# A scatter of expert results in fp32r with a skipped second group, and four weight subtractions moved to VectorE

## The chip, the cores and the metric

The kernel runs on one core of a Trainium2 chip. The metric is the device time of one execution in microseconds (us); the time of a kernel is the median of several executions.

## The reference

A decoder trunk of two layers over one sequence of 256 tokens with 1024 channels, in fp32. Layer 0 is an input projection into q, k, v, a recurrent branch and its gate; differential attention with partial rotary embedding; a causal convolution with a gated linear recurrence; an output projection; and a dense SwiGLU of width 2816. Layer 1 is a pooling mixer and a mixture of eight SwiGLU experts of width 3584, of which each token uses two. The change concerns how the experts' results come back to their tokens:

```python
def moe_swiglu(h, router_w, wg, wu, wd):
    t = h.reshape(-1, dm)
    top_val, top_idx = lax.top_k((t @ router_w).astype(jnp.float32), TOP_K)
    gates = jax.nn.softmax(top_val, axis=-1)
    combine = jnp.sum(jax.nn.one_hot(top_idx, N_EXPERTS) * gates[..., None], axis=1)
    out = jnp.zeros_like(t)
    for e in range(N_EXPERTS):
        he = jax.nn.silu(t @ wg[e]) * (t @ wu[e])
        out = out + (combine[:, e:e + 1] * he) @ wd[e]
```

The result is the RMS norm of h plus this, times a gain.

## The kernel before

The weights are streamed in pieces of 128 partitions by 2048 columns (1 MB) by SyncE's DMA queue into a rotating set of buffers; `load_free` (L145) issues the next loads as soon as a buffer has been read for the last time.

**Layer 0, 0 to 330 us.** Matmuls of f32 weights run in three fp32r products: each half of a piece is split into hi (rounded to fp32r) and lo (the rest), `split_half` (L159): ScalarE makes hi (L167), and lo = raw - hi is a subtraction on VectorE or GpSimd (L168). `on_pool` (L155) chooses: the second halves (a = 1) of pieces 0 to 16 go to GpSimd where a caller doesn't name an engine, all others to VectorE. Pieces 0 to 9 are those of the input projection. Tile names in the order's rows carry a number: lo_197 is the second half of piece 1, lo_245 that of piece 2, lo_564 of piece 7, lo_629 of piece 8. The engines' instructions run in the order in which the program writes them (a schedule by hand), each engine its own queue, with semaphores between them.

Beside these products the first 107 us hold a chain of small steps. The row norms: squares on ScalarE, nine steps on 128x2 tiles on VectorE (`finish_rs`: L243, L223 to L230), `dg` (L283) for TensorE's `rsr` (L288), then `xb` (L402), the convolution (L409), the recurrence's gates (L419, L426), `lru_a` to `lru_d` (L436 to L450: GpSimd's product at L438, VectorE's at L442 and L446, scans at L450), the rotary products `rt` and `qk` (L464 to L468), transposes `qkT` (L477) and their copies to qT and kT (L480), then attention (scores from L494 on).

**Layer 1's experts, 330 to 1159 us.** Eight experts in seven pieces each, n = 7e + p. An expert's tokens lie in slots: a first group of 64 (`C0`), a second of 32 (`C1`); where an expert has more than 64 tokens, `big[e]` is set, read into a register of TensorE's queue. In piece n, TensorE runs the gate and up products of the first group (`mg`, L969, f32 tiles 128x64), under `tc.If(big[e])` those of the second group (`go`, L980, and `yo`, L1024, tiles of 128x32), else a matmul of one column (L991, bf16, so that the bank has a writer), then the down products of piece n - 1 (`y`, L1014) and transposes (`tp`, L1003). One piece reads six loads of 1 MB.

**The scatter.** After an expert's last piece `results(e)` (L1027) copies the sums of the second group (`yo`, VectorE) and the first (`y_`, ScalarE) to SBUF, into `ysb`. `gates(e)` (L938) builds for each token a row that holds its gate value at its slot (`selg`); `scatter_a` (L1031) transposes it (four 128x128) and copies it to `selT`. `scatter_b(t)` (L1042), for each half t of the tokens, multiplies the selection with the results, f32, 512 columns, in two row groups of 64 partitions (j = 0, 1, one for each half of the channels, each in its own bank), first the second group (m = 1), then the first (m = 0): four pairs. TensorE reads each f32 matmul as two instructions, so a call counts eight. `scatter_c` (L1049) adds the banks to the running output `ho` on VectorE. A table of jobs places these calls: gates and `scatter_a` in pieces 7e + 4 and 7e + 5, the two calls of expert e - 1's scatter in pieces 7e + 1 and 7e + 2 of the next expert, behind the first products of the piece (L1114 to L1119). There are 14 calls in the loop; the last expert's two stand behind the last down product (L1170), and behind them the final norm (`norm_out`, L1157): squares on ScalarE, nine small steps, four products on VectorE (L1167), four stores. `selg`, `selT` and `ysb` share one 1 MB buffer, `yt`.

Of the kernel before, what the change touches and what calls it, by code (L numbers as in the profile page):

```python
# [18 lines left out]
P = 128  # L19
# [8 lines left out]
E = 8  # L28
# [29 lines left out]
def hybrid_kernel(ctx, tc, x, cst, prm, row, gate, rtr, w_in, w_out, w_gu, w_dn, w_pool, m_gu, m_dn, out):  # L58
# [96 lines left out]
    def on_pool(i, a):  # L155

        return a and i < 17
# [757 lines left out]

    def more_room():


        yt = late.tile([P, W], F32, tag="band", name="yt")
        late_room.update(ysb=yt[:, 0:1024].rearrange("p (a c) -> p a c", a=2), selT=yt[:, 1024:1536].rearrange("p (a s) -> p a s", a=2),  # L920
                         selg=yt[:, 1536:2048].rearrange("p (t m s) -> p t m s", t=NT, m=2))
# [16 lines left out]
    def gates(e):  # L938
        for t in range(NT):
            for m, (a, c) in enumerate(((0, C0), (C0, C1))):  # L940
                dve.tensor_scalar(late_room["selg"][:, t, m].rearrange("p (o s) -> p o s", s=c),
                                  iota[:, a:a + c].rearrange("p (o s) -> p o s", o=1).to_broadcast([P, P // c, c]),
                                  pos[:, t, e:e + 1], cmb[:, t, e:e + 1], op0=OP.is_equal, op1=OP.mult)
# [38 lines left out]

    def more(parts):

        for e in sorted({n // EP for _, n in parts}):
            with tc.If(big[e] > 0, preferred_fallthrough_block=True) as c:
                for f, n in parts:
                    if n // EP == e:
                        f(n)
            with c.Else():  # L990
                pe.matmul(go[0:C1, 511:512], idb[:, 0:C1], idb[:, 0:1], start=True, stop=True)  # L991

    def hidden_a(n, b):
        sg = work.tile([P, 3, P], F32, name="sg", bufs=2)
        for v_, g_ in ((sg[:, 0:2], gates_of(b)), (sg[:, 2:3], gates_of(go[:, 0:2 * P]))):
            act.activation(v_, g_[:, :, 0, :], AF.Silu)  # L996
            dve.tensor_tensor(v_, v_, g_[:, :, 1, :], op=OP.mult)  # L997
        return sg

    def hidden_b(n, sg):  # L1000
        b = bank2("tp", "tp")
        for i in range(3):
            pe.transpose(b[:, i * P:(i + 1) * P], sg[:, i, :], ident)  # L1003
        het[n] = work.tile([P, 3, P], F32, name="het", bufs=2)
        act.copy(het[n].rearrange("p a c -> p (a c)"), b[:, 0:3 * P])  # L1005
# [21 lines left out]
    def results(e):  # L1027
        dve.tensor_copy(late_room["ysb"][:, 1], yo)
        act.copy(late_room["ysb"][:, 0], y_[e])

    def scatter_a():  # L1031

        b = misc("st")
        for t in range(NT):
            for m in range(2):
                pe.transpose(b[:, m * S + t * P:m * S + (t + 1) * P], late_room["selg"][:, t, m], ident)
        dve.tensor_copy(late_room["selT"].rearrange("p a s -> p (a s)"), b)
# [4 lines left out]
    def scatter_b(t, room=lambda name: misc(name)):  # L1042
        bs = [room(f"sc{t}{j}") for j in range(2)]
        for m in (1, 0):
            for j in range(2):
                pe.matmul(bs[j], late_room["selT"][j * C0:(j + 1) * C0, m, t * P:(t + 1) * P], late_room["ysb"][j * C0:(j + 1) * C0, m], start=m == 1, stop=m == 0)  # L1046
        return bs
# [41 lines left out]
    def scatter_next(t):  # L1089
        sc_[t] = scatter_b(t)  # L1090
# [14 lines left out]
    for e in range(E):  # L1105
        n = e * EP
        if e:
            do(n - 4, 2, gather_a, e)
            do(n - 3, 1, gather_next, e, 0)
            do(n - 3, 3, gathered, e, 0)  # L1110
            do(n - 2, 1, gather_next, e, 1)
            do(n - 2, 3, gathered, e, 1)
            do(n, 1, load_big, e)
            do(n + 1, 1, scatter_next, 0)  # L1114
            do(n + 1, 3, scattered, e - 1, 0)
            do(n + 2, 1, scatter_next, 1)
            do(n + 2, 3, scattered, e - 1, 1)
        do(n + 4, 0, gates, e)
        do(n + 5, 1, scatter_a)  # L1119
# [51 lines left out]
    bs = [scatter_b(0), scatter_b(1, lambda name: bank2("gu", name, 2))]  # L1171
# [10 lines left out]
    def rest_of(e, r):  # L1182
# [4 lines left out]
        for t in range(NT):  # L1187
            dve.tensor_scalar(s_[:, t, :], iota, pos[:, t, bass.ds(e, 1)], -float(CAP + r * P), op0=OP.subtract, op1=OP.is_equal)
            dve.tensor_scalar(late_room["selg"][:, t, 0], s_[:, t, :], cmb[:, t, bass.ds(e, 1)], None, op0=OP.mult)
# [4 lines left out]
        for t in range(NT):  # L1194
            pe.transpose(b[:, t * P:(t + 1) * P], late_room["selg"][:, t, 0], ident)
        dve.tensor_copy(late_room["selT"][:, 0], b[:, 0:S])
        with tc.For_i(0, EP, 1) as p:
# [7 lines left out]
            for c in range(2):  # L1205
                w = whole(m_dn[(e * EP + p) * 2 + c])
                sg = work.tile([P, 3, P], F32, tag="sg", name="sgo", bufs=2)[:, 0:2]
# [6 lines left out]
                ht = work.tile([P, 3, P], F32, tag="het", name="hto", bufs=2)[:, 0:2]  # L1214
                act.copy(ht, b[:, 0:2 * P].rearrange("p (a c) -> p a c", a=2))
                for j in range(2):
# [3 lines left out]
                    dve.tensor_add(y[:, j], y[:, j], b)  # L1220
        for t in range(NT):
            for j in range(2):
                b = misc(f"so{j}")
                pe.matmul(b, late_room["selT"][:, 0, t * P:(t + 1) * P], y[:, j], start=True, stop=True)
                hv = ho[0][:, t, j * 512:(j + 1) * 512]
                dve.tensor_add(hv, hv, b)
# [110 lines left out]
```

## Time and profile before

| | us |
|---|---|
| median of 3 runs (lowest, highest) | 1176.07 (1175.68, 1177.18) |
| profiled execution | 1175.88 |
| its span in the trace | 1173.9 |
| TensorE busy (share of the span) | 1133.8 (97%) |
| VectorE busy | 295.3 (25%) |
| ScalarE busy | 242.9 (21%) |
| GpSimd busy | 98.4 (8%) |
| chain of waits, by engine | TensorE 74%, DMA 18%, VectorE 4%, ScalarE 3% |

The profiled execution's time is 2.0 us longer than its span: what lies before the first and after the last instruction. Shares are averages over stages with different limits; the table by stages, the chain of waits and the timelines below separate them. In the rows, PE is TensorE, PEld its weight loads, DVE is VectorE, ACT ScalarE, POOL GpSimd; an arrow from a bracket names what ended the idle time before an instruction.

### The profile page before, as it was taken

The numbers are of one execution on the slowest core, as the hardware profiler recorded it, in microseconds if no ns is written. First come the engines' busy times: TensorE is split into PE (matmuls) and PEld (weight loads), VectorE is DVE, ScalarE is ACT, GpSimd is POOL, SyncE is SP. The second block draws the span as 40 slices with busy tenths as digits, with TensorE's granted clock in tenths as the row PEclk, the third lists the DMA queues.
The fourth block names the chain that finished last, engine by engine and source line by source line (L and its number), as shares of the span: only waits on it lengthen the run. The fifth ranks groups of instructions, "written<-read, shape, count | busy, mean of one in ns | idle before, by whom it ended". The sixth has DMA issues, their size and how long they took to land.

```text
span 1173.9 us, 16811 instructions
## 1 busy us (share of the span) xinstructions
PE 1133.8 (97%) x7071; PEld 582.5 (50%) x7071; DVE 295.3 (25%) x572; ACT 242.9 (21%) x491; POOL 98.4 (8%) x114
## 2 busy tenths in 40 slices
PE   7989999999999999998989999999999999999995
PEld 6867999999853333322323343333334433443331
DVE  6686664444731011111101100110010011001112
ACT  5756544444510010000000000000000000000011
POOL 2723151121200000000000000000000000000000
PEclk9999999999999999999999999999999999999998
DMA  9434956555899999999999999999999999999981
GB/s 353 149 124 141 391 182 213 173 187 180 306 372 415 419 415 419 416 416 419 415 421 415 418 415 415 419 402 420 416 418 407 415 421 415 419 363 417 418 350 38
DMA packets 69774, 408.67 MB, mean 348 GB/s; under 512 B 7844, under 2 KB 8104, under 8 KB 31400
## 3 DMA queue, kind: packets, MB, share of 16 engines
q1 hardware_dynamic: 69528, 407.08, 86.8%
q8 instruction: 80, 1.31, 0.5%
q10 hardware_dynamic: 144, 0.10, 0.1%
q14 instruction: 22, 0.18, 0.0%
HBM read 406.10 MB, written 1.05 MB: 347 GB/s over the span
## 4 chain that ended last, share of the span: by engine, by line
PE 74%; DMA 18%; DVE 4%; ACT 3%; issue 1%; DVEq 0%; ACTq 0%; SPq 0%
PE mg L969 26%; PE y L1014 12%; PE gu L185 11%; DMA raw<-in_m_gu 10%; PE go L980 6%; PE dn L185 5%; PE yo L1024 3%; DMA twohi<-in_m_gu 3%; DMA twolo<-in_m_gu 2%; PE sc L1046 2%; PE xe L951 2%; PE tp L1003 2%; DMA sparehl<-in_m_gu 1%; PE wo L185 1%; DMA spareh<-in_m_gu 1%; ACT hi L167 1%
## 5 line engine op out<-in xcount | busy, mean ns | idle before, releaser
L969 PE MATMUL mg<-raw,xe 128*64 128x512 f32 x928 | 219.0, 601 | 6.7 <-DMA raw<-in_m_gu 6.5
L997 DVE TENSOR_TENSOR sg<-sg,mg 128x256 f32<-128x256 f32 x56 | 23.6, 421 | 576.7 <-ACT sg L996 576.7
L996 ACT ACTIVATE sg<-mg 128x256 f32<-128x256 f32 x56 | 21.5, 383 | 564.7 <-PE mg L969 564.7
L168 DVE TENSOR_TENSOR lo<-raw,hi 128x1024 fp32r<-128x1024 f32 x80 | 99.9, 1269 | 95.6 <-ACT hi L167 95.4
L969 PEld LDWEIGHTS mg<-raw,xe 128*64 128x64 f32 x928 | 59.7, 136 | 123.1 <-issue 98.8
L167 ACT ACTIVATE hi<-raw 128x1024 fp32r<-128x1024 f32 x96 | 98.7, 1051 | 43.1 <-PE dn L185 28.5
L1014 PE MATMUL y<-raw,het 128*64 128x512 f32 x432 | 99.1, 593 | 1.1 <-DMA raw<-in_m_dn 1.1
L1014 PEld LDWEIGHTS y<-raw,het 128*64 128x64 f32 x432 | 30.7, 137 | 64.2 <-issue 57.0
L1005 ACT COPY het<-tp 128x384 f32<-128x384 f32 x56 | 26.8, 478 | 169.3 <-PE tp L1003 169.3
L969 PE MATMUL mg<-twohi,xe 128*64 128x512 f32 x212 | 55.2, 604 | 0.7 <-DMA twohi<-in_m_gu 0.7
L969 PE MATMUL mg<-twolo,xe 128*64 128x512 f32 x212 | 55.5, 602 | 0.4 <-DMA twolo<-in_m_gu 0.4
L1014 PE MATMUL y<-twohi,het 128*64 128x512 f32 x120 | 54.8, 593 | 0.5 <-ACT het L1005 0.5
L1014 PE MATMUL y<-twolo,het 128*64 128x512 f32 x120 | 54.7, 593 | 0.2 <-DMA twolo<-in_m_dn 0.2
L185 PE MATMUL gu<-xfl,hi 128*128 128x256 f32 x352 | 50.3, 283 | 0.0
L185 PE MATMUL gu<-xfh,hi 128*128 128x256 f32 x352 | 50.1, 283 | 0.0
L185 PE MATMUL gu<-xfh,lo 128*128 128x256 f32 x352 | 50.1, 283 | 0.0
L185 PEld LDWEIGHTS gu<-xfh,hi 128*128 128x128 f32 x352 | 46.2, 191 | 0.9
L185 PEld LDWEIGHTS gu<-xfl,hi 128*128 128x128 f32 x352 | 45.7, 192 | 0.2 <-DVE xfl L270 0.2
L185 PEld LDWEIGHTS gu<-xfh,lo 128*128 128x128 f32 x352 | 45.7, 192 | 0.0
L168 POOL TENSOR_TENSOR lo<-raw,hi 128x1024 fp32r<-128x1024 f32 x16 | 39.2, 2455 | 71.4 <-ACT hi L167 54.9
L969 PE MATMUL mg<-spare,xe 128*64 128x512 f32 x168 | 41.3, 602 | 2.7 <-DMA spare<-in_m_gu 2.7
L980 PE MATMUL go<-raw,xe 128*32 128x256 f32 x704 | 41.8, 380 | 0.0
(378 smaller groups left out, 1378.2 us busy)
## 6 DMA issues: line engine op xcount, KB each, us to landing
raw<-in_m_gu SPq DMA_DIRECT2D x116, 1024.0 KB, 17.8
raw<-in_m_dn SPq DMA_DIRECT2D x54, 1024.0 KB, 18.7
twohi<-in_m_gu SPq DMA_DIRECT2D x53, 512.0 KB, 13.8
twolo<-in_m_gu SPq DMA_DIRECT2D x53, 512.0 KB, 12.6
raw<-in_w_gu SPq DMA_DIRECT2D x22, 1024.0 KB, 4.8
spare<-in_m_gu SPq DMA_DIRECT2D x21, 1024.0 KB, 15.7
twohi<-in_m_dn SPq DMA_DIRECT2D x30, 512.0 KB, 13.8
twolo<-in_m_dn SPq DMA_DIRECT2D x30, 512.0 KB, 12.3
```

Of the source, the lines that this page charges most:

```text
L167: act.activation(hi, r, AF.Copy)
L168: eng.tensor_tensor(lo, r, hi.bitcast(F32), op=OP.subtract)
L185: pe.matmul(dst, l, r, start=start, stop=stop)
L951: pe.matmul(v_[:, k], h[:, t, (4 * k4 + k) * P:(4 * k4 + k + 1) * P], s_[:, t, :], start=t == 0, stop=t == NT - 1)
L969: pe.matmul(b[c * C0:(c + 1) * C0], x_[:, k, 0:C0], block(MOE[n] + k // 2, (k % 2 * 2 + c) * 512), start=k == 0, stop=k == 1)
L980: pe.matmul(go[q:q + C1, 0:2 * P], x_[:, k, C0:CAP], block(MOE[n] + k // 2, (k % 2 * 2 + c) * 512 + r * 2 * P, 2 * P), start=k == 0, stop= ...
L997: dve.tensor_tensor(v_, v_, g_[:, :, 1, :], op=OP.mult)
L1003: pe.transpose(b[:, i * P:(i + 1) * P], sg[:, i, :], ident)
L1005: act.copy(het[n].rearrange("p a c -> p (a c)"), b[:, 0:3 * P])
L1014: pe.matmul(y_[e][j * C0:(j + 1) * C0], het[n][:, r, c * C0:(c + 1) * C0], block(DOWN[n] + c, (2 * j + r) * 512), start=p == c == r == 0, ...
L1024: pe.matmul(yo[q:q + C1], het[n][:, 2, (2 * c + r) * C1:(2 * c + r + 1) * C1], block(DOWN[n] + c, (2 * j + r) * 512), start=p == r == 0, s ...
L1046: pe.matmul(bs[j], late_room["selT"][j * C0:(j + 1) * C0, m, t * P:(t + 1) * P], late_room["ysb"][j * C0:(j + 1) * C0, m], start=m == 1, s ...
```

## The change

Two independent edits.

1. `on_pool` no longer takes pieces 1, 2, 7 and 8: four subtractions go from GpSimd's queue to VectorE's, in the place where `split_half` is called.
2. The scatter. The selection `selT` becomes an exact 0 or 1 in fp32r (`is_gt` of the transposed gate rows); each slot's gate value is a sum over its row (`gsl`). `results` multiplies y by it and makes an fp32r hi half (ScalarE) and lo half (VectorE, `halve` at L209). `scatter_b` multiplies in fp32r, one instruction for a matmul: first group hi, then, under an If on `big[e]`, second group hi and lo, else the matmul of one column, then first group lo. `selg` and `selT` move to a pool of their own, `ysb` takes all of `yt`, and `sg` and `het` go from two buffers to one. The path for experts of more than 96 tokens changes in the same way (left out below).

```diff
     def on_pool(i, a):
 
-        return a and i < 17
+        return a and i < 17 and i not in (1, 2, 7, 8)
...
+    selg = work.tile([P, NT, 2, P], F32, name="selg", bufs=1)
+    selT = work.tile([P, 2, S], F32R, name="selT", bufs=1)
+
     def more_room():
 
-
-        yt = late.tile([P, W], F32, tag="band", name="yt")
-        late_room.update(ysb=yt[:, 0:1024].rearrange("p (a c) -> p a c", a=2), selT=yt[:, 1024:1536].rearrange("p (a s) -> p a s", a=2),
-                         selg=yt[:, 1536:2048].rearrange("p (t m s) -> p t m s", t=NT, m=2))
+        late_room.update(ysb=late.tile([P, W], F32R, tag="band", name="yt").rearrange("p (u a c) -> p u a c", u=2, a=2))
...
+    def where_big(e, f):
+        with tc.If(big[e] > 0, preferred_fallthrough_block=True) as c:
+            f()
+        with c.Else():
+            pe.matmul(go[0:C1, 511:512], idb[:, 0:C1], idb[:, 0:1], start=True, stop=True)
+
...
     def hidden_a(n, b):
-        sg = work.tile([P, 3, P], F32, name="sg", bufs=2)
+        sg = work.tile([P, 3, P], F32, name="sg", bufs=1)
...
-        het[n] = work.tile([P, 3, P], F32, name="het", bufs=2)
+        het[n] = work.tile([P, 3, P], F32, name="het", bufs=1)
...
     def results(e):
-        dve.tensor_copy(late_room["ysb"][:, 1], yo)
-        act.copy(late_room["ysb"][:, 0], y_[e])
-
-    def scatter_a():
+        for m, b in ((1, yo), (0, y_[e])):
+            hi, lo = (late_room["ysb"][:, u, m] for u in range(2))
+            halve(hi, lo, b, gsl[e][:, m:m + 1])
+
+    gsl = {}
+
+    def scatter_a(e):
 
         b = misc("st")
         for t in range(NT):
             for m in range(2):
-                pe.transpose(b[:, m * S + t * P:m * S + (t + 1) * P], late_room["selg"][:, t, m], ident)
-        dve.tensor_copy(late_room["selT"].rearrange("p a s -> p (a s)"), b)
+                pe.transpose(b[:, m * S + t * P:m * S + (t + 1) * P], selg[:, t, m], ident)
+        gsl[e] = work.tile([P, 2], F32, name="gsl", bufs=2)
+        dve.tensor_reduce(gsl[e], b.rearrange("p (a s) -> p a s", a=2), axis=AX.X, op=OP.add)
+        dve.tensor_scalar(selT.rearrange("p a s -> p (a s)"), b, 0.0, None, op0=OP.is_gt)
...
-    def scatter_b(t, room=lambda name: misc(name)):
+    def scatter_b(e, t, room=lambda name: misc(name)):
         bs = [room(f"sc{t}{j}") for j in range(2)]
-        for m in (1, 0):
+
+        def part(m, u, start=False, stop=False):
             for j in range(2):
-                pe.matmul(bs[j], late_room["selT"][j * C0:(j + 1) * C0, m, t * P:(t + 1) * P], late_room["ysb"][j * C0:(j + 1) * C0, m], start=m == 1, stop=m == 0)
+                rows_ = slice(j * C0, (j + 1) * C0)
+                pe.matmul(bs[j], selT[rows_, m, t * P:(t + 1) * P], late_room["ysb"][rows_, u, m], start=start, stop=stop)
+
+        part(0, 0, start=True)
+        where_big(e, lambda: [part(1, u) for u in range(2)])
+        part(0, 1, stop=True)
         return bs
```

The first two of the four subtractions on VectorE, the difference between the orders (- before, + after), near the start:

```order
 L270 SCALAR_TENSOR_TENSOR xml<-xt_171,pr,xmh 128x256 x2
 L168 TENSOR_TENSOR lo_189<-raw_97,hi_188 128x1024
+L168 TENSOR_TENSOR lo_197<-raw_97,hi_196 128x1024
 L243 SCALAR_TENSOR_TENSOR nwt<-ssq 128x2
 L223 TENSOR_SCALAR rs<-nwt 128x2
...
 L283 TENSOR_SCALAR dg<-pr,rs 128x128 x2
 L168 TENSOR_TENSOR lo_229<-raw_103,hi_228 128x1024
+L168 TENSOR_TENSOR lo_245<-raw_103,hi_244 128x1024
 L402 TENSOR_TENSOR xb<-x_155,rsr 128x256
 L402 TENSOR_TENSOR xb<-x_156,rsr 128x256
```

lo_197 now stands ahead of the nine small steps of the row norm (left out between them), lo_245 ahead of the first channels of the recurrent branch; in both places GpSimd's queue loses the same row. The other two, around the copies of q and k (`th`, `cv`: the recurrence; `rt`: the rotary products):

```order
 L480 COPY qT<-qkT_546 128x512
+L168 TENSOR_TENSOR lo_564<-raw_264,hi_563 128x1024
 L442 SCALAR_TENSOR_TENSOR th<-ri,th 128x1024
 L464 TENSOR_TENSOR rt<-qk,cs 128x128
...
 L446 TENSOR_TENSOR cv<-cv,th 128x1024
+L168 TENSOR_TENSOR lo_629<-raw_343,hi_628 128x1024
 L450 SCALAR_TENSOR_TENSOR th<-la,cv 128x256 x4
```

lo_564 stands ahead of both rotary products of k, lo_629 between them and the scans. TensorE's queue at the first scatter call of the loop, in the kernel after (before, the four L1046 matmuls of sc stand between the same mg rows, with no branch):

```order
L970 MATMUL mg_4189<-raw_3880,xe_3407 64x512 x2
L1055 MATMUL sc_4192<-yt,selT 128x512
L1055 MATMUL sc_4193<-yt,selT 128x512
L985 COMPARE_AND_BRANCH
L1055 MATMUL sc_4192<-yt,selT 128x512
L1055 MATMUL sc_4193<-yt,selT 128x512
L1055 MATMUL sc_4192<-yt,selT 128x512
L1055 MATMUL sc_4193<-yt,selT 128x512
L985 UNCONDITIONAL_BRANCH
L988 LDWEIGHTS idb
L988 MATMUL go<-idb 32x1
L985 UNCONDITIONAL_BRANCH
```

Either the four matmuls behind the compare run or the one of L988; the last pair (the lo half of the first group) and the next mg products follow behind the last row.

## Rows read from the trace of the kernel before

**Rows 1.** Table by stages: stretch, length, busy us by engine, clock, DMA share, GB/s.

```profile
0.00:107.00 107.00, 94.99 (x519) 79.21 (x520) 77.08 (x132) 69.33 (x141) 46.54 (x56) 0.97 0.55 197
107.00:330.00 223.00, 222.79 (x1554) 206.71 (x1552) 126.01 (x193) 106.48 (x162) 51.85 (x59) 0.99 0.65 234
...
739.00:826.00 87.00, 85.59 (x407) 29.85 (x406) 10.82 (x28) 7.73 (x22) 0.00 (x0) 1.00 1.01 414
826.00:1020.00 194.00, 193.59 (x1512) 74.40 (x1514) 18.53 (x48) 12.35 (x35) 0.00 (x0) 1.00 1.01 416
```

**Rows 2.** Chain of waits, pieces in order of time: start us, us, what.

```profile
145.04 5.62 PE dn L185 x24
...
826.41 1.94 PE mg L969 x8
...
837.87 1.92 PE sc L1046 x8
...
856.33 1.92 PE sc L1046 x8
```

**Rows 3.** Waits of TensorE, 0 to 107 us: total us, times, longest.

```profile
PE rsr L288 <- DVE dg L283: 2.9, 1, 2.9
PE qkT L477 <- DVE qk L468: 2.7, 1, 2.7
```

**Rows 4.** VectorE, timeline 16.9 to 25.2 us: start us, us, instruction, [idle before].

```profile
18.09 0.16 DVE L227 SCALAR_TENSOR_TENSOR nwt<-rs 128x2 f32<-128x2 f32 x1
18.29 2.26 DVE L228 TENSOR_TENSOR nwt<-nwt 128x2 f32<-128x2 f32 x1
...
23.08 0.48 DVE L283 TENSOR_SCALAR dg<-pr,rs 128x128 f32<-128x128 f32 x2
23.48 1.22 DVE L168 TENSOR_TENSOR lo<-raw,hi 128x1024 fp32r<-128x1024 f32 x1
25.06 0.43 DVE L402 TENSOR_TENSOR xb<-x,rsr 128x256 f32<-128x256 f32 x1 [0.37 <-ACT rsr L289]
```

**Rows 5.** Timeline of GpSimd (POOL), 16.9 to 64.9 us.

```profile
18.10 4.73 POOL L168 TENSOR_TENSOR lo<-raw,hi 128x1024 fp32r<-128x1024 f32 x2 [17.27 <-ACT hi L167]
...
53.48 3.40 POOL L438 TENSOR_TENSOR cv<-cv,ri 128x1024 f32<-128x1024 f32 x1
...
61.02 2.34 POOL L168 TENSOR_TENSOR lo<-raw,hi 128x1024 fp32r<-128x1024 f32 x1 [0.82 <-ACT hi L167]
```

**Rows 6.** Timeline of VectorE, 53 to 72 us.

```profile
57.89 2.46 DVE L464 TENSOR_TENSOR rt<-qk,cs 128x128 f32<-128x128 f32 x1
...
60.86 0.28 DVE L464 TENSOR_TENSOR rt<-qk,cs 128x128 f32<-128x128 f32 x1
61.06 2.52 DVE L467 TENSOR_TENSOR rt<-qk,cs 128x64 f32<-128x64 f32 x2
```

**Rows 7.** Timeline of ScalarE, 10 to 26 us.

```profile
16.98 2.93 ACT L167 ACTIVATE hi<-raw 128x1024 fp32r<-128x1024 f32 x3
```

**Rows 8.** Timeline of TensorE's weight loads (PEld), 1094.4 to 1096.6 us.

```profile
1094.50 0.30 PEld L1046 LDWEIGHTS sc<-yt 64*128 64x128 f32 x4 [0.81 <-issue]
...
1096.41 0.20 PEld L969 LDWEIGHTS mg<-raw,xe 128*64 128x64 f32 x4 [0.76 <-issue]
```

**Rows 9.** The same view, 1099.4 to 1103 us.

```profile
1100.76 0.14 PEld L969 LDWEIGHTS mg<-raw,xe 128*64 128x64 f32 x2 [0.28 <-issue]
1101.71 0.09 PEld L991 LDWEIGHTS <-idb 128*32 128x32 bf16 x1 [0.81 <-issue]
1101.82 0.20 PEld L969 LDWEIGHTS mg<-raw,xe 128*64 128x64 f32 x4
```

**Rows 10.** Timeline of ScalarE from 1158 us on.

```profile
1158.69 0.58 ACT L1029 COPY yt<-y 128x512 f32<-128x512 f32 x1 [3.75 <-PE y L1014]
```

**Rows 11.** Timeline of VectorE from 1158 us on.

```profile
1160.59 1.28 DVE L1054 TENSOR_TENSOR ho<-ho,sc 128x512 f32<-128x512 f32 x2 [5.39 <-PE sc L1046]
1162.31 1.28 DVE L1054 TENSOR_TENSOR ho<-ho,sc 128x512 f32<-128x512 f32 x2 [0.43 <-PE sc L1046]
```

More of the change, by code (lines that the diff above doesn't have):

```diff
@@ L940, in gates @@
             for m, (a, c) in enumerate(((0, C0), (C0, C1))):
-                dve.tensor_scalar(late_room["selg"][:, t, m].rearrange("p (o s) -> p o s", s=c),
+                dve.tensor_scalar(selg[:, t, m].rearrange("p (o s) -> p o s", s=c),
                                   iota[:, a:a + c].rearrange("p (o s) -> p o s", o=1).to_broadcast([P, P // c, c]),
@@ L981, in gate_up_more @@
                               start=k == 0, stop=k == KD - 1)
+    def where_big(e, f):
[3 more added lines that the diff above has]
+            pe.matmul(go[0:C1, 511:512], idb[:, 0:C1], idb[:, 0:1], start=True, stop=True)
     def more(parts):
         for e in sorted({n // EP for _, n in parts}):
[L986 to L991, printed above, removed]
+            where_big(e, lambda: [f(n) for f, n in parts if n // EP == e])
     def hidden_a(n, b):
-        sg = work.tile([P, 3, P], F32, name="sg", bufs=2)
+        sg = work.tile([P, 3, P], F32, name="sg", bufs=1)
         for v_, g_ in ((sg[:, 0:2], gates_of(b)), (sg[:, 2:3], gates_of(go[:, 0:2 * P]))):
@@ L1087, in gathered, with scatter_next @@
         gather_c(xe[e % 2], k4, gb_[k4])
-    def scatter_next(t):
-        sc_[t] = scatter_b(t)
+    def scatter_next(e, t):
+        sc_[t] = scatter_b(e, t)
     def scattered(e, t):
@@ L1113, in hybrid_kernel @@
             do(n, 1, load_big, e)
-            do(n + 1, 1, scatter_next, 0)
+            do(n + 1, 1, scatter_next, e - 1, 0)
             do(n + 1, 3, scattered, e - 1, 0)
-            do(n + 2, 1, scatter_next, 1)
+            do(n + 2, 1, scatter_next, e - 1, 1)
             do(n + 2, 3, scattered, e - 1, 1)
         do(n + 4, 0, gates, e)
-        do(n + 5, 1, scatter_a)
+        do(n + 5, 1, scatter_a, e)
     do(N - 1, 1, late_gains)
@@ L1170, in hybrid_kernel @@
     results(E - 1)
-    bs = [scatter_b(0), scatter_b(1, lambda name: bank2("gu", name, 2))]
+    bs = [scatter_b(E - 1, 0), scatter_b(E - 1, 1, lambda name: bank2("gu", name, 2))]
     for t in range(NT):
@@ L1188, in rest_of @@
             dve.tensor_scalar(s_[:, t, :], iota, pos[:, t, bass.ds(e, 1)], -float(CAP + r * P), op0=OP.subtract, op1=OP.is_equal)
-            dve.tensor_scalar(late_room["selg"][:, t, 0], s_[:, t, :], cmb[:, t, bass.ds(e, 1)], None, op0=OP.mult)
+            dve.tensor_scalar(selg[:, t, 0], s_[:, t, :], cmb[:, t, bass.ds(e, 1)], None, op0=OP.mult)
             dve.tensor_scalar(s_[:, t, :], s_[:, t, :], rs1[:, t:t + 1], None, op0=OP.mult)
@@ L1194, in rest_of @@
         for t in range(NT):
-            pe.transpose(b[:, t * P:(t + 1) * P], late_room["selg"][:, t, 0], ident)
-        dve.tensor_copy(late_room["selT"][:, 0], b[:, 0:S])
+            pe.transpose(b[:, t * P:(t + 1) * P], selg[:, t, 0], ident)
+        gs = work.tile([P, 2], F32, tag="gsl", name="gso", bufs=2)
+        dve.tensor_reduce(gs[:, 0:1], b[:, 0:S], axis=AX.X, op=OP.add)
+        dve.tensor_scalar(selT[:, 0], b[:, 0:S], 0.0, None, op0=OP.is_gt)
         with tc.For_i(0, EP, 1) as p:
@@ L1206, in rest_of @@
                 w = whole(m_dn[(e * EP + p) * 2 + c])
-                sg = work.tile([P, 3, P], F32, tag="sg", name="sgo", bufs=2)[:, 0:2]
+                sg = work.tile([P, 3, P], F32, tag="sg", name="sgo", bufs=1)[:, 0:2]
                 g_ = gates_of(bs[c])
@@ L1213, in rest_of @@
                     pe.transpose(b[:, i * P:(i + 1) * P], sg[:, i, :], ident)
-                ht = work.tile([P, 3, P], F32, tag="het", name="hto", bufs=2)[:, 0:2]
+                ht = work.tile([P, 3, P], F32, tag="het", name="hto", bufs=1)[:, 0:2]
                 act.copy(ht, b[:, 0:2 * P].rearrange("p (a c) -> p a c", a=2))
@@ L1220, in rest_of @@
                     dve.tensor_add(y[:, j], y[:, j], b)
+        halve(late_room["ysb"][:, 0], late_room["ysb"][:, 1], y, gs[:, 0:1])
         for t in range(NT):
@@ L1223, in rest_of @@
                 b = misc(f"so{j}")
-                pe.matmul(b, late_room["selT"][:, 0, t * P:(t + 1) * P], y[:, j], start=True, stop=True)
+                for u in range(2):
+                    pe.matmul(b, selT[:, 0, t * P:(t + 1) * P], late_room["ysb"][:, u, j], start=u == 0, stop=u == 1)
                 hv = ho[0][:, t, j * 512:(j + 1) * 512]
```

## The prediction, before the changed kernel ran

> **What bounds the kernel now.** The page says that TensorE has work for nearly the whole span, so the first question is where that work is the limit and where it merely fits beside something else. The table by stages answers it [rows 1]: from 107 to 330 us TensorE has work in 222.79 of 223.00 us at 0.65 of the DMA engines, so that a microsecond saved in the stage before arrives at 330 unchanged. From 739 to 826 us and on to 1020 the DMA share is above 1.00, at 414 to 416 GB/s: there the weights come as fast as they can. The chain of waits then says where the one limit takes over from the other [rows 2]: its last DMA piece ends at 826.41, and from there to the end it is TensorE with a short tail on ScalarE and VectorE. What TensorE saves ahead of 826 it spends waiting for the same bytes; what it saves behind 826 counts in full. The same view prices the two kinds of matmul: the f32 scatter call of eight takes 1.92 us, and 24 fp32r matmuls of 512 columns in L185 take 5.62 us, which is 0.234 each. Last, the waits of TensorE in the first 107 us name only two long ones on VectorE, 2.9 us at rsr (L288) and 2.7 us at qkT (L477) [rows 3]; the timelines of VectorE and GpSimd show why.
>
> **Part one: four subtractions from GpSimd to VectorE.** At 18.09 us a 128x2 step of the rms chain takes 0.16 us; the next, at 18.29, takes 2.26, and the one behind it as much, so that dg (L283), for which TensorE waits, starts at 23.08 [rows 4]. GpSimd runs two L168 subtractions from 18.10 for 4.73 us [rows 5]; by the order these are lo_197 and lo_245. The pattern comes back at 57.89 us, where one 128x128 product takes 2.46, and at 61.06, where two of 128x64 take 2.52, while the 128x128 product at 60.86 takes 0.28 [rows 6]; the next two subtractions of GpSimd, lo_564 and lo_629, lie over them, the second from 61.02 [rows 5]. So four blocks of 2.1 to 2.2 us leave VectorE's line, and four subtractions of 1.22 us (unblocked, as at 23.48 [rows 4]) enter it.
>
> Step by step: (a) lo_197 now stands ahead of nwt (L243) and adds a wait on ScalarE: its hi half is the first of three that start at 16.98 and take 2.93 [rows 7], done near 18.0. Queued behind the waiting instruction are the rms steps, dg, and with it TensorE. It runs from 18.1 to 19.3, nine small steps at 0.2 follow, and dg starts at 21.1 instead of 23.08: 2.0 earlier. (b) lo_245 stands ahead of xb (L402): 21.1 + 0.4 (dg) + 1.22 (lo_229) + 1.22 = 24.0 against 25.06: xb is 1.1 earlier. TensorE's wait at rsr shrinks by 2.0; the convolution behind xb, which feeds the gates and the long row of activations on ScalarE ahead of qT, gains only 1.1. (c) lo_564 stands behind GpSimd's own L438 (53.48, 3.40 us [rows 5]), which will block it as it now blocks L442; it costs 1.22, and two blocks of 2.2 go: qk (L468), for which qkT waits, comes 1.1 + 4.4 - 1.2 = 4.3 earlier at the most. (d) lo_629 takes 1.22 again, ahead of the scans and of the copy of kT: from there the lead is 3.1. What is late next is the attention behind kT, which waits for VectorE and ScalarE; GpSimd's later subtractions stay as they are. I take **3.0 us** for this part. The upper end is both waits of rows 3 less what (a) leaves, 2.0 + 2.7 = 4.7; the lower end is the lead of xb alone, 1.1, should something else hold kT back. The lead goes through 107 to 330 unchanged; behind that each load is issued when a buffer comes free, so that the stretch bound by DMA moves as a whole.
>
> **Part two: the scatter.** A call spans 1.92 us from its first weight load (1094.50) to the next one of mg (1096.41) [rows 8]: 0.10 until the first matmuls, four pairs (two row groups side by side) at 0.43, and 0.10 before tiles of another shape may load. The new call has fp32r pairs. Taking 0.234 for a pair, as for one matmul of L185, a call of an expert with a second group is 0.10 + 4 x 0.234 + 0.10 = 1.14, which is 0.78 less. Without one it is the pair for hi, the tiny matmul of the Else, and the pair for lo. The same filler in L991 costs 0.10 for the change of shape and 0.11 until the next load (1100.76 to 1101.71 is two pairs plus 0.10, then 1101.82 [rows 9]), so the call is 0.43 + 0.11 + 0.43 = 0.97, which is 0.95 less. Behind 826 lie six calls in the loop: two of an expert without the second group (837.87 and 856.33 [rows 2]) and four of experts with one, the last at 1094.50 [rows 8]; the rows of go (L980) say which experts those are. 2 x 0.95 + 4 x 0.78 = **5.0 us**. Does the first of them run into a late load? Two pieces with a call are 856.33 - 837.87 = 18.5 us apart, while six loads of 1 MB (6.29 million bytes) at 416 GB/s take 15.1. The lead over the loads, nothing at 826.41, is thus some 3 us when the first call ends, and 0.95 is taken from it. The eight calls ahead of 826 gain nothing: the loads of the stretches at a full DMA share cover them, and without that cover they would give up to 0.95 each.
>
> No row shows fp32r in tiles of 64 rows. If its two row groups ran one behind the other, a call would be 0.97 + 0.47 = 1.44 or 1.14 + 0.94 = 2.08: 2 x 0.48 - 4 x 0.16 = 0.3 us. I take side by side, since the nearest row, the f32 pair in the same tiles, runs so; 0.3 stays as the lower end.
>
> Each call now crosses an If. The filler's rows hold the crossing of the If in each piece as well, and beyond the change of shape they show nothing for it: at 1101.71 the compare has been worked off ahead of the matmuls. [...]
>
> **Part three: the tail.** The last call waits for ScalarE's copy of y, from 1158.69 for 0.58 [rows 10], and the first addition starts at 1160.59 [rows 11]. Now hi takes that copy's place; lo follows on VectorE for some 0.65 (as one addition of rows 11), to about 1160.0, beside the hi pair and the filler; the lo pair ends near 1160.45, and the second tile's by 1161.1 instead of 1162.31. The four additions then run without the pause of 0.43, but the squares on ScalarE behind them take up part of it: **0.3 us**, with 0.5 and -0.7 (hi, lo and filler all in series) as ends.
>
> The added halves in the loop (two activations for one, two subtractions for one copy, per expert) sit on engines that have work for a tenth of that time [rows 1], and TensorE asks for them a piece later. The single buffers of sg and het cost nothing: the transposes and products that read the old content stand earlier on TensorE. Without that cover each would be a wait of some 0.5 us per piece.
>
> **Sum:** 3.0 + 5.0 + 0.3 = 8.3 us. The profiled execution took 1175.88, 0.2 below the median of 1176.07; on the median that is 1167.8 us.
>
> **Rivals.** (1) The row groups of fp32r don't overlap: 3.0 + 0.3 + 0.3 = 3.6, so 1172.5. For it: fp32r occurs nowhere in such tiles. Against: f32 pairs overlap fully [rows 8]. (2) VectorE becomes the bound of the first stage: what the blocks give back goes to the subtractions and to ScalarE's row, and part one is worth 0 to 0.5: 1170.6. For it: VectorE has work in 77 of the first 107 us [rows 1]. Against: 8.7 us of blocks go and 4.9 of work come. [...] (3) The loads bind behind 826 as well, and part two is worth nothing: 1172.8. Against: the lead of 3 us. (4) **Slower:** the If in the middle of a call has one pair ahead of it where the If of a piece has a dozen, and TensorE's queue runs dry there. From (8.3 + 2.4) / 8 = 1.3 us for a crossing on, the eight crossings (six, and two at the end) make the kernel slower; at 2 us it is 16 - 8.3, so 1183.8. For it: no row shows an If under so little work. Against: the crossings that are shown cost nothing [rows 9].
>
> **Chances.** Forecast 0.60, (1) 0.13, (2) 0.13, (3) 0.07, (4) 0.07, of which half is slower by over 0.2% (2.4 us, what a measurement of this kernel can tell from no change). The low end takes the upper ends, 4.7 + 5.0 + 0.5 = 10.2, so 1165.9, and 0.4 for the spread of the runs: 1165.5. The high end takes in (1) to (3): 1173.0. Faster 0.88: the forecast, (2), and most of (1) and (3), which lie 0.9 to 1.2 inside the bound of 1173.7. Same 0.08, slower 0.04.
>
> **What would show it.** Right: no 128x2 step over 0.2 us between 18 and 21 us; dg at about 21.1; the wait at qkT under 0.5; the same TensorE work 3 us earlier at 330; scatter calls of about 1.0 and 1.15 us; no DMA in the chain behind about 823. Wrong: a call of 1.4 us or more (1), dg or kT as late as now (2), waits on DMA behind 826 (3), a gap at the If (4).

## The result and the profile after

| | before | after |
|---|---|---|
| median, us (runs; lowest, highest) | 1176.14 (4; 1175.68, 1177.18) | 1168.46 (4; 1165.94, 1168.91) |
| profiled execution, its span | 1175.88, 1173.9 | 1168.91, 1166.8 |

The ratio of after to before is 0.9925, with a 95% interval of 0.9912 to 0.9938: faster, by 7.7 us between the medians (8.8 by the ratio), where 8.3 were forecast. The time lies in the range, 0.7 us over the forecast. How it comes about is less tidy than the sum: one term came out larger, one as worked out, and two stretches at a granted clock of 0.50 took part of it back in the execution that was profiled. One execution of the kernel before, beside the last experiments, took 1636.21 us at a granted clock of 0.65 and is in no comparison.

The table by stages of the changed kernel, cut where the work is the same as in [rows 1] (columns as there):

```profile
0.00:102.00 102.00, 91.63 (x520) 75.16 (x521) 73.32 (x136) 69.43 (x141) 35.31 (x52) 0.98 0.56 207
102.00:325.00 223.00, 222.10 (x1554) 206.29 (x1551) 126.04 (x193) 106.41 (x162) 51.81 (x59) 1.00 0.65 235
...
823.00:1020.00 197.00, 197.00 (x1592) 76.80 (x1590) 20.92 (x51) 13.64 (x37) 0.00 (x0) 1.00 1.02 417
```

The first stage is 5 us shorter for the same work (0.9 of it the start of this execution, see below). GpSimd is busy 11.2 us less in it and VectorE 3.8 less, although it took over four subtractions: what it no longer spends blocked is more than it got. The waits of TensorE in the first 107 us, answering to [rows 3]:

```profile
PE qkT L477 <- DVE qk L468: 2.0, 2, 1.5
...
PE rsr L288 <- DVE dg L283: 0.8, 1, 0.8
```

Of 2.9 us at rsr 0.8 are left, and qkT's longest wait on VectorE fell from 2.7 to 1.5 (2.0 in all). VectorE's timeline at the place of [rows 4]:

```profile
17.20 1.23 DVE L168 TENSOR_TENSOR lo<-raw,hi 128x1024 fp32r<-128x1024 f32 x1 [2.60 <-ACT hi L167]
...
19.52 0.16 DVE L228 TENSOR_TENSOR nwt<-nwt 128x2 f32<-128x2 f32 x1
...
20.11 0.48 DVE L283 TENSOR_SCALAR dg<-pr,rs 128x128 f32<-128x128 f32 x2
20.50 2.35 DVE L168 TENSOR_TENSOR lo<-raw,hi 128x1024 fp32r<-128x1024 f32 x2
22.77 0.75 DVE L402 TENSOR_TENSOR xb<-x,rsr 128x256 f32<-128x256 f32 x2
```

lo_197 stands at 17.20 and waits for ScalarE's hi half; the 128x2 steps behind it take 0.16 us each, none 2.26, and dg starts at 20.11 instead of 23.08. ScalarE's first square was at 14.09 us before and at 13.23 now, ahead of any of the moved subtractions: 0.86 of every lead in this stage is the start of this one execution (in the second trace of the changed kernel that square stands at 14.30). dg's own gain is 2.1. The place of [rows 6], with both other subtractions:

```profile
52.51 2.83 DVE L168 TENSOR_TENSOR lo<-raw,hi 128x1024 fp32r<-128x1024 f32 x1
55.26 1.21 DVE L442 SCALAR_TENSOR_TENSOR th<-ri,th 128x1024 f32<-128x1024 f32 x1
56.40 0.28 DVE L464 TENSOR_TENSOR rt<-qk,cs 128x128 f32<-128x128 f32 x1
...
57.19 0.28 DVE L464 TENSOR_TENSOR rt<-qk,cs 128x128 f32<-128x128 f32 x1
...
60.26 1.22 DVE L168 TENSOR_TENSOR lo<-raw,hi 128x1024 fp32r<-128x1024 f32 x1
...
63.74 0.67 DVE L480 COPY kT<-qkT 128x512 f32<-128x512 f32 x1
```

lo_564 takes 2.83 us instead of 1.22 while GpSimd's L438 runs from 50.86 for 3.40; behind it L442 takes 1.21 where it took 2.39, and both rotary products 0.28. The three qkT matmuls that started at 64.06 start at 58.22, and the copy of kT at 63.74 instead of 68.57.

The chain of waits where the experts begin and where the loads stop binding, answering to [rows 2]:

```profile
325.20 6.07 PE xe L952 x32
331.27 6.16 PE mg L970 x28
...
822.85 1.94 PE mg L970 x8
...
1135.42 7.00 PE mg L970 x24
```

The gather products (xe) began at 330.27 before, so the lead was 5.07 at 325.20; but they took 4.00 us then and 6.07 now, and the first expert products are only 3.0 earlier (331.27 against 334.27). The last load ends at 822.85 instead of 826.41: 3.6. Two calls of the scatter in the same chain, first for an expert without a second group:

```profile
834.31 0.42 PE sc L1055 x2
834.74 0.11 PE go L988
834.84 0.43 PE sc L1055 x2
835.27 2.73 PE mg L970 x12
```

And, in the chain of a later stretch, for an expert with one:

```profile
955.85 1.13 PE sc L1055 x8
```

0.96 and 1.13 us instead of 1.92. Behind 823 no wait on DMA is left in the waits of TensorE. Six such calls are 5.1 us, yet the last down products began at 1154.99 before and begin at 1148.07 now, 6.9 earlier, which is 3.4 more than at 823: the 24 mg matmuls at 1135.42 took 7.00 us, where 24 take 5.30 elsewhere. The table by stages in steps of 2 us shows the clock there, and around the router:

```profile
322.00:324.00 2.00, 1.31 (x13) 1.04 (x13) 1.64 (x9) 0.00 (x0) 0.00 (x0) 0.79 0.99 418
324.00:326.00 2.00, 1.94 (x13) 1.34 (x12) 0.93 (x5) 0.82 (x2) 0.00 (x0) 0.50 1.02 430
326.00:328.00 2.00, 2.00 (x11) 2.00 (x11) 0.00 (x0) 0.09 (x1) 0.00 (x0) 0.50 1.00 422
328.00:330.00 2.00, 2.00 (x12) 2.00 (x11) 0.56 (x1) 0.00 (x0) 0.00 (x0) 0.51 1.01 426
...
1136.00:1138.00 2.00, 2.00 (x8) 0.65 (x6) 0.00 (x0) 0.04 (x1) 0.00 (x0) 0.50 0.18 63
```

The same steps of the kernel before:

```profile
326.00:328.00 2.00, 2.00 (x17) 1.81 (x18) 1.54 (x10) 0.00 (x0) 0.00 (x0) 0.82 1.00 410
328.00:330.00 2.00, 2.00 (x15) 1.22 (x13) 1.74 (x10) 0.00 (x0) 0.00 (x0) 0.50 0.99 418
330.00:332.00 2.00, 1.94 (x16) 1.73 (x14) 0.15 (x1) 0.91 (x2) 0.00 (x0) 0.83 1.04 438
```

The granted clock was 0.50 from about 323 to 330 us now, and from about 327 to 331 before; in the steps beside it (320 to 322 and 330 to 332 us now) it was 1.00. The tail, answering to [rows 10, 11]:

```profile
1152.49 0.75 DVE L216 SCALAR_TENSOR_TENSOR yt<-y,gsl,yt 128x512 fp32r<-128x512 f32 x1 [3.10 <-ACT yt L215]
1153.84 2.48 DVE L1067 TENSOR_TENSOR ho<-ho,sc 128x512 f32<-128x512 f32 x4 [0.59 <-PE sc L1055]
```

hi took 0.69 us on ScalarE, lo 0.75 here; the first addition starts 2.71 us behind the last pair of y (1151.13), where it started 2.54 behind it (1158.05). The four additions then run through, and the last products (L1167, now L1180) are 8.33 behind that pair instead of 8.44.

The books of this execution, in us of lead over the profiled one of the kernel before: 0.9 at the start, 5.1 at the end of the dense SwiGLU, 3.0 at the first expert product (2.1 lost at half clock), 3.6 at 823, 6.9 at the last down products (5.1 from the calls, 1.7 lost at half clock), 7.0 at the end.

### The profile page after: what moved, and what is told of

Same layout as the page of the kernel before. It is cut to its first block, busy times and chain, and to the rows that moved or that the text cites. A ratio compares the mean times of both kernels' runs of the same rounds, so it can differ in the third digit from the quotient of the medians.

```text
span 1166.8 us, 16799 instructions
## 1 busy us (share of the span) xinstructions
PE 1122.3 (96%) x7040; PEld 578.4 (50%) x7041; DVE 303.2 (26%) x592; ACT 248.0 (21%) x499; POOL 87.1 (7%) x110
## 4 chain that ended last, share of the span: by engine, by line
PE 68%; DMA 23%; DVE 4%; ACT 3%; issue 1%; DVEq 0%; ACTq 0%; SPq 0%
PE mg L970 23%; PE gu L185 11%; PE y L1016 11%; DMA raw<-in_m_gu 8%; PE go L981 6%; PE dn L185 5%; PE yo L1026 3%; DMA raw<-in_m_dn 3%; DMA twohi<-in_m_gu 3%; DMA twolo<-in_m_dn 2%; PE xe L952 2%; DMA spare<-in_m_gu 2%; PE tp L1005 1%; DMA twolo<-in_m_gu 1%; DMA spare<-in_m_dn 1%; DMA sparehl<-in_m_gu 1%
## 5 line engine op out<-in xcount | busy, mean ns | idle before, releaser
L970 PE MATMUL mg<-raw,xe 128*64 128x512 f32 x928 | 221.9, 606 | 9.6 <-DMA raw<-in_m_gu 9.3
L168 DVE TENSOR_TENSOR lo<-raw,hi 128x1024 fp32r<-128x1024 f32 x84 | 106.2, 1285 | 97.7 <-ACT hi L167 97.6
L1005 PEld LDWEIGHTS tp<-pr,sg 128*128 128x128 f32 x168 | 17.4, 141 | 46.4 <-issue 44.6
```

Of the source, the lines that this page charges most:

```text
L168: eng.tensor_tensor(lo, r, hi.bitcast(F32), op=OP.subtract)
L970: pe.matmul(b[c * C0:(c + 1) * C0], x_[:, k, 0:C0], block(MOE[n] + k // 2, (k % 2 * 2 + c) * 512), start=k == 0, stop=k == 1)
```

## The experiments

Each time is compared with runs of the kernel before on the same chip, by the ratio of after to before with its 95% interval; "us faster" is the share that the ratio lies below 1, times the median of before. It isn't the ratio of the two medians, and the two can differ by over 1 us: by the medians the four subtractions alone are 3.7 us faster and pieces 1 and 2 alone 3.3. The kernel before had medians of 1177.4 to 1178.3 on these chips, and single executions from 1174.5 to 1179.3; its one trace, of 1175.88 us, lies in the faster part of that spread.

| | ratio | us faster |
|---|---|---|
| four subtractions alone | 0.9975 (0.9964 to 0.9985) | 2.9 (1.8 to 4.2) |
| pieces 1 and 2 alone | 0.9984 (0.9972 to 0.9996) | 1.9 (0.5 to 3.3) |
| pieces 7 and 8 alone | 0.9978 (0.9967 to 0.9989) | 2.6 (1.3 to 3.9) |
| scatter alone | 0.9965 (0.9952 to 0.9977) | 4.1 (2.7 to 5.7) |
| scatter in f32 under an If, four subtractions | 0.9942 (0.9926 to 0.9958) | 6.8 (4.9 to 8.7) |
| changed kernel without the If | 0.9923 (0.9909 to 0.9938) | 9.1 (7.3 to 10.7) |
| changed kernel, first and second time | 0.9932 and 0.9920 | 8.0 and 9.4 |
| changed kernel, filling 14 and 8, twice | 0.9913 and 0.9915 | 10.2 and 10.0 |
| changed kernel, filling 14 and 4 | 0.9901 (0.9886 to 0.9917) | 11.7 (9.8 to 13.4) |
| kernel before, filling 14 and 8 | 0.9996 (0.9987 to 1.0005) | 0.5 (-0.6 to 1.5) |

**The four subtractions alone.** In the kernel before:

```diff
-        return a and i < 17
+        return a and i < 17 and i not in (1, 2, 7, 8)
```

> The kernel before with the four subtractions on VectorE and nothing else. Theory: these four are worth what the changed kernel shows at 305 us, a lead of 5.0, less the 0.9 us by which its profiled execution was ahead at 13 us, before any of the four: some 4.2 us, of which the stretch bound by DMA returns what it gets, so 1171 to 1173 us. It shows dg 2 us or more earlier and no wait of 2.5 us at qkT. Rival: the lead is mostly the better start of one execution, or the stretch bound by DMA takes it; then 1174 us or more. Second rival: the stretch at half the granted clock from 323 to 330 us, which in the changed kernel is twice as long as before, comes with this part; then the lead at the first expert product is 2 us smaller than at 305 us.

1173.64 us against 1177.37, 2.9 us by the ratio. Its trace has dg at 20.15, the lead of 5.0 at the dense SwiGLU (0.8 of it the start), the gather products at 325.24 for 5.85 us and from there on a lead of 3.2 to 3.3 to the end. The first theory was too high by 1.3, and the second rival fits where the rest went in this trace: the same stretch at half clock as in the changed kernel. That the subtractions bring that stretch isn't shown; the scatter alone, below, has a longer one without them.

**Pieces 1 and 2 alone, then 7 and 8 alone**, in the same line: `i not in (1, 2)` and `i not in (7, 8)`.

> The kernel before with only the subtractions of pieces 1 and 2 on VectorE. Theory: two of the four blocks go, in the rms chain; dg comes 2 us earlier, xb and what hangs on it 1.1 to 1.7, and the wait at qkT stays at 2 to 3 us: a gain of 1.5 to 1.8 us at 305 us, so 1174.4 us. Rival: the whole gain of part one comes from TensorE not idling at rsr; then 1172 us, as with all four. Second rival: the gain at rsr is lost again at qkT, which waits for ScalarE anyway; then 1176 us.

> The kernel before with only the subtractions of pieces 7 and 8 on VectorE. Theory: the blocks at L464 and L467 go, two of 2.2 us, against 1.2 us of work ahead of qk and 1.2 us more ahead of the scans; the stall at rsr with its 2.9 us stays. The trace with pieces 1 and 2 alone was 1.3 us ahead at the first product of the dense SwiGLU (after taking off its better start of 0.8), all four 4.2; this one should be 2.4 to 2.9 ahead, and 1.5 to 2.9 us faster than before. Rival: pieces 1 and 2 bring all that arrives at the end, because both are worth 1.9 to 2.9 us by the times so far; then no difference from before.

1.9 and 2.6 us faster. The waits of TensorE in the first 107 us tell the two apart by place. With pieces 1 and 2 moved:

```profile
PE qkT L477 <- DVE qk L468: 2.6, 1, 2.6
PE qkT L477 <- ACT hi L167: 2.5, 1, 2.5
...
PE rsr L288 <- DVE dg L283: 1.4, 1, 1.4
```

With 7 and 8 moved:

```profile
PE rsr L288 <- DVE dg L283: 3.4, 1, 3.4
...
PE qkT L477 <- DVE qk L468: 0.5, 1, 0.5
```

With 1 and 2 moved the wait at rsr falls to 1.4 and that at qkT stays at 2.6; with 7 and 8 moved rsr has 3.4 (2.9 before) and qkT's wait on VectorE falls to 0.5. The blocked steps go with them: the first still has L464 with 2.44 and L467 with 2.50 us, the second L228 with 2.25. By the times both gains reach the end (the rival, that pieces 1 and 2 bring all of it, falls). The traces say so only of pieces 1 and 2: their lead is 2.1 at the gather products and 2.2 at the last pair of y, 0.8 of it the start; with 7 and 8 it is 3.5 at the gather products, which then take 6.36 us, and 0.9 at the last pair of y, 0.8 of it the start. The intervals are too wide to say whether the parts add up to the 2.9 of all four.

**The scatter alone.** The changed kernel with `return a and i < 17`.

> The changed kernel with the four subtractions left on GpSimd: the scatter alone. Theory: six shorter calls behind the DMA-bound stretch (2 x 0.96 less than 1.92, 4 x 1.14 less) and the tail give 5.0 + 0.2 to 0.3, so 1170.8 us; if the drop of the granted clock at 1135 us, which cost 1.7 us in the changed kernel, comes with the scatter, 1172.5 us. Rival: the calls save nothing because the loads bind; then 1176 us. The calls are to read 0.96 and 1.14 us in the chain in either case.

1173.09 us, 4.1 faster. A call of a small expert in its chain runs from 840.15 to 841.12, 0.97 us again. TensorE's timeline at the gather products, at the first go product behind the last load, and at the last pair of y:

```profile
329.83 6.85 PE L952 MATMUL xe<-selr,h 128*128 128x96 f32 x32
...
830.57 1.71 PE L981 MATMUL go<-raw,xe 128*32 128x256 f32 x28
...
1155.28 0.59 PE L1016 MATMUL y<-twohi,het 128*64 128x512 f32 x1
```

The last two of these in the kernel before:

```profile
828.29 1.93 PE L980 MATMUL go<-raw,xe 128*32 128x256 f32 x32
...
1158.05 0.59 PE L1014 MATMUL y<-twohi,het 128*64 128x512 f32 x1
```

Its execution came to the experts late (the gather products took 6.85 us, the first expert product started at 336.61 against 334.20): 2.3 late behind the last load, and 2.8 early at the last pair of y. That is 5.05 us gained behind the last load, the 5.0 of the working; the second trace of the changed kernel, with no drop of the clock in this stretch, has the same 5.05. The 4.1 of the times (2.7 to 5.7) agrees with it.

**The scatter in f32 under an If**, with the four subtractions and the gate left in the selection:

```diff
-        for m in (1, 0):
-            for j in range(2):
-                pe.matmul(..., start=m == 1, stop=m == 0)
...
+        with tc.If(big[e] > 0, preferred_fallthrough_block=True) as c:
+            part(1, True, False)
+            part(0, False, True)
+        with c.Else():
+            part(0, True, True)
```

> The kernel before with the four subtractions on VectorE and a scatter that stays in f32 with the gate in the selection, but crosses an If: both groups where the expert has a second, else the first alone. Theory: fp32r is the larger part of the scatter's gain: here calls of small experts are 1.05 us (0.10 + 2 x 0.43 + 0.10) and those with a second group still 1.92, so 1.7 us behind 826 us in place of 5.0; with the 2.9 us of the subtractions 4.6 us faster than before, ratio 0.996. Rival: the skipped second group is the larger part; then it comes within 1 us of the changed kernel, ratio 0.993 to 0.994.

6.8 us faster, and the interval (4.9 to 8.7) leaves out the 4.6 expected; where the rest comes from isn't shown (its trace leads by 4.9 at the last pair of y, 0.7 of it the start). The changed kernel's 8 to 9.4 are not far off: by the times the two theories can't be parted. The trace can. In its chain, a call of an expert without a second group:

```profile
834.69 1.06 PE sc L1047 x4
```

And of one with it:

```profile
956.42 1.92 PE sc L1047 x8
```

1.06 and 1.92, as worked out; from the first go product behind the last load (825.11) to the last pair of y (1153.16) it gained 1.7 on before, where the scatter alone, in fp32r, gained 5.05. So leaving out the second group, with f32 kept, brings about a third of the gain behind 823.

**Without the If.** The changed kernel with

```diff
-        where_big(e, lambda: [part(1, u) for u in range(2)])
+        for u in range(2):
+            part(1, u)
```

> The changed kernel with the second group's two fp32r products in every call, without the If. Theory: the If costs nothing but the filler's 0.1 us with its changes of shape, so a call of a small expert is 1.14 us instead of 0.96 and one with a second group 1.14 as before: 0.4 us longer, which the times can't tell. Rival: crossing the If costs time that the calls hide in the trace but not in the total (one pair of matmuls ahead of it); then this kernel is 1 us or more faster than the changed one.

A call of a small expert in its chain, now with both groups:

```profile
835.05 1.12 PE sc L1055 x8
```

1168.6 us, ratio 0.9923: the same as the changed kernel on the other chips, within some 1.7 us either way. The crossing costs nothing that shows, and the skipped products save 0.16 us a call of a small expert, nothing that the times could tell. With fp32r in place, the If is not what makes the difference: six calls at 1.12 to 1.13 instead of 1.92 save some 4.8 of the 5.1 us.

**The changed kernel again**, unchanged, twice, on two chips.

> The changed kernel as it is, for its spread and a second trace. Theory: the two drops of the granted clock to one half, 323 to 330 us and 1135 to 1138 us, come and go from execution to execution; then the times scatter over 2 to 3 us (1165.9 to 1168.9) and the second trace lacks one of them or has it elsewhere. Rival: they belong to the kernel's order of work; then both stand at the same places again and the times lie within 1 us.

> The changed kernel once more, beside the two with other filling. Theory: gather products of 5.8 to 6.1 us again in its trace, as in the two traces of it so far, and a median 1.5 to 2 us above the one with filling on both sides. Rival: the length of that stretch is chance; then 4.0 us may stand here as well, and the medians differ by less than 1 us.

1168.36 (1167.47 to 1169.79) and 1168.65 (1167.09 to 1169.93). Neither trace has a drop at 1135 us: that one belongs to its execution, not to the kernel. Both have the one at the router, with gather products of 6.03 and 6.54 us; with the first trace that is three of three. So the expectation that both come and go was half wrong.

**More filling at the router.** The kernels run matmuls of no use there, 8 ahead of the wait for the router's mask and 4 behind it:

```diff
-WARM = (8, 4, 8)
+WARM = (14, 8, 8)
```

> The changed kernel with more matmuls of no use around the router's small steps near 322 to 325 us (14 ahead of the wait and 8 behind it in place of 8 and 4), so that TensorE is not idle there. Theory: the drop of the granted clock to one half at 323 us, which lasts 3 to 10 us in the traces so far and makes the 32 gather products take 4.0 to 6.1 us and more, follows the short matmuls and the idle of 0.7 us ahead of it; with the gap filled it is shorter or gone, the gather products take some 3 to 4 us, and the kernel is 1 to 3 us faster than the changed one and scatters less. Rival: the drop comes from the router's short matmuls, or from nothing that the order of work sets; then it stands as before and the time is the same or 0.5 us longer.

> The changed kernel with filling on both sides (14 and 8), beside the others on one chip. Theory: 1.5 to 2 us faster than the changed kernel, gather products of 3.8 to 4 us. Rival: as for the changed kernel beside it, within 1 us.

> The changed kernel with only the filling ahead of the wait lengthened (14 and 4). Theory: the idle of 0.7 us ahead of the slot products is what lengthens the stretch at half the clock, so this does as well as both together: 1166.7 us, gather products of 4 us. Rival: the four more behind the wait do it, by keeping TensorE going until the selection is ready; then 1168.4 us and gather products of 6 us.

> The kernel before with the longer filling around the router's steps (14 and 8 matmuls in place of 8 and 4). Theory: what the filling gives is independent of the change: the gather products behind it take 3.8 to 4.0 us here too, and the times lie 1 to 2 us under those of before and scatter less. Rival: only the changed kernel, which comes to the router 5 us earlier, has the long stretch at half the clock; then no difference, or 0.5 us more for the longer filling.

With 14 and 8 the changed kernel takes 1166.66 on the chip of the If experiments and 1167.90 on the last one, 0.75 under the changed kernel beside it, where 1.5 to 2 were expected: by the time the rival holds (within 1 us); with 14 and 4 it takes 1166.41 (1164.79 to 1167.91) there, 2.2 under it. TensorE's timeline over the filling (warm), the gather products and the first mg products, with 14 and 4:

```profile
322.30 2.48 PE L89 MATMUL warm<-cs 128*128 128x256 bf16 x14
...
325.83 4.09 PE L952 MATMUL xe<-selr,h 128*128 128x96 f32 x32
329.85 4.51 PE L970 MATMUL mg<-raw,xe 128*64 128x512 f32 x20
```

The same in the changed kernel beside it:

```profile
323.15 1.87 PE L89 MATMUL warm<-cs 128*128 128x256 bf16 x8
...
326.09 6.54 PE L952 MATMUL xe<-selr,h 128*128 128x96 f32 x32
332.57 1.94 PE L970 MATMUL mg<-raw,xe 128*64 128x512 f32 x8
```

And with 14 and 8 beside them:

```profile
323.06 3.15 PE L89 MATMUL warm<-cs 128*128 128x256 bf16 x14
...
328.10 3.87 PE L952 MATMUL xe<-selr,h 128*128 128x96 f32 x32
331.91 2.37 PE L970 MATMUL mg<-raw,xe 128*64 128x512 f32 x10
```

With more filling the gather products take 3.8 to 4.1 us in all four traces, partly because now the filling runs at 0.50 in their place: in the last of these, where the drop began at 322 us and lasted 7, they begin at 328.10, and the experts at 331.91, little ahead of the 332.57 without it. In the first trace with 14 and 8 the drop lasted some 3.5 us and the experts began at 330.49; with 14 ahead alone at 329.85. So the filling hides the drop, and whether it also shortens it is open: the same kernel had a short one and a long one. In the kernel before the longer filling gave nothing (0.9996, 0.9987 to 1.0005): in its trace the gather products took 4.00 us already, and with the longer filling they take 3.81 and begin 1.4 later. The theory that the filling is worth the same with and without the change falls; why it is so rests on one trace of each. The kernel with 14 and 4 is the fastest here; it was timed four times, the two spreads overlap, and its lead over the changed kernel is likely, not settled.

## Why the prediction was right, and where it was not

**Part one: the size was right, and in part by luck: two errors offset each other.** Alone it is worth 2.9 us by the times, 3.0 was taken, with 1.1 to 4.7 as ends. Step (a), dg 2.0 earlier: 2.1. Step (b), xb 1.1 earlier: 25.06 to 22.77 less the 0.86 of the start is 1.4, and 1.7 at the convolution behind it (L409, 27.15 to 24.57). Step (c), at most 4.3 for qkT: 5.0 (58.22 against 64.06, less 0.86). The two blocks gave 4.4 and lo_564 took 1.1, as worked out; the lead from (b), 1.7 where 1.1 was put, is the term that was too small. Step (d), 3.1 from kT on: 4.0, and 4.2 at the end of the dense SwiGLU. The wait at qkT, under 0.5 as a sign, is 1.5 and 0.5: TensorE itself comes to it 3.2 us earlier (its matmuls ahead of it end at 55.96 instead of 59.17, 0.9 of it the start). The working also took TensorE's durations as they were; but behind the waits of 2.9 and 2.7 us the matmuls of before ran at half the clock (0.50 from about 23.5 to 26.9 us and from 64.5 to 67.9; the first eight at 24.26 us took 2.05 us, the same eight take 1.20 now), while the trace of the changed kernel has no such stretch between 13 and 323 us:

```profile
24.00:26.00 2.00, 2.00 (x11) 2.00 (x11) 1.45 (x3) 1.35 (x3) 1.01 (x1) 0.50 0.94 393
```

How much of the larger leads comes from this isn't shown. The step that failed is **"the lead goes through 107 to 330 unchanged"**: TensorE's full share made it look safe, and up to 325 us it held, but against the one trace of the kernel before 2.1 us were lost again in the gather products at half the clock, and such long products (5.85 to 6.54 us) stand in all three traces of the changed kernel and in the four subtractions alone. Whether the change brings them is open: the scatter alone, whose early stage is that of before, has 6.85. In the step from 326 to 328 us TensorE is busy for 2.00 of 2.00 us at a clock of 0.50; the busy share alone does not tell the two clocks apart.

**Part two: as worked out.** 0.96 for 0.97, 1.13 for 1.14, 5.05 us between the last load and the last down product in the scatter alone. The value taken for what no row showed, fp32r pairs in tiles of 64 rows side by side, was right: four pairs in 1.13 us, less 0.10 at either end, are 0.23 each. The lead of 3 us over the loads was enough; no wait on DMA stands behind 823. The eight calls ahead of it gained little or nothing that arrives: the lead is 3.0 at 331 and 3.6 at 823, and in the scatter alone it is -2.4 and -2.3.

**Branches.** The filler and the crossing take 0.11 us in the changed kernel too, with one pair ahead of it: the call is 0.43 + 0.11 + 0.42 us of matmuls and changes of shape. The compares of L985 take 65 to 364 ns in its trace, 179 at the median of 110; the last one ahead of the call at 834.31 starts at 833.6 and takes 212, done before the call's first weight load (834.24). Six crossings at that median, if they lay in the open, would cost an estimated 1.1 us; the chain doesn't show it, and the times, the same without the If to within some 1.7 us, could not tell it.

**The tail** gave 0.1 where 0.3 was taken. The terms that were too small are lo, 0.75 us where an addition's 0.65 was put, and hi, 0.69 against the copy's 0.58; the additions begin 0.17 later and win back 0.3 by running through.

**The rivals.** (1) falls with 1.13 us for four pairs. (2) falls: the stage gained. The reverse, a subtraction on GpSimd that takes longer beside an instruction of VectorE, already stood in the trace of the kernel before. GpSimd's timeline has there:

```profile
56.84 3.36 POOL L168 TENSOR_TENSOR lo<-raw,hi 128x1024 fp32r<-128x1024 f32 x1
```

This is lo_564, 3.36 us where GpSimd's other subtractions take 2.3 to 2.5: VectorE's L442, from 55.57 for 2.39, was still running when it started. In these pairs the one that starts later takes longer: L442, behind L438 from 53.48 for 3.40, takes 2.39 and in the changed kernel, with L438 done, 1.21; why is not shown. None of the four moved subtractions held up GpSimd in the changed kernel (L438 takes 3.40 us in both traces, and beside the other three GpSimd runs nothing); lo_564 was itself blocked once, by L438, but it took the place of L442, which was blocked there before, so that it cost 1.1 us and not 2.8. (3) falls with the waits on DMA, of which none is left behind 823. (4) falls with the kernel without the If.

## What to carry to other kernels

A small step on VectorE that takes about as long as the GpSimd operation beside it (here 2.26 us for a step of 0.16) may be blocked by it, not slow, and moving that operation to VectorE can shorten VectorE's own line (busy 73.3 us of the first stage here, 77.1 before). Price a saving by the stage it lies in: in the stretch where the loads bind a shorter call gave next to nothing (the lead went from 3.0 to 3.6 us over eight calls in the changed kernel), behind it the whole of it (5.05 us for six in the scatter alone). And follow a lead past the next stretch in which TensorE has little to do: the same 32 products cost from 4.0 to 6.9 us here, according to how long the granted clock was at 0.50.

## What the hardware showed that was not expected

Behind the router's 32 products of 8 columns, or while they run, the granted clock falls to 0.50 in every trace, for 3 to 4 us in some and 7 to 10 in others: the 32 gather products behind them took 4.00 us in the kernel before and 4.02 with pieces 1 and 2 moved, and 5.80 to 6.85 in the other eight traces with the same filling, among them the scatter alone, whose early stage is that of before. What decides between them is open.

The wait at rsr cost more than itself: in or behind it (2.9 to 3.4 us) the clock falls to 0.50 in all four traces with pieces 1 and 2 on GpSimd, for 3 us or more, and in none of the ten with them on VectorE, where that wait is 0.5 to 1.5 us.

Two further drops, at 545 us (under the loads) and at 1135 us, stood in one trace of the changed kernel and not in the two others, and the second cost 1.7 us: a difference of 1.5 to 2 us between two single executions here needs no cause in the code.
